# A two-layer decoder on one core: one more plain pair in block two, output rows for accumulating DMAs rounded in place in two buffers, and another order of the last pair's products

## The chip, the cores and the metric

The kernel runs on one core of a Trainium2 chip. The metric is the device time of one execution in microseconds (us), from several runs of the same program; lower is better. The engines are named as the profile names them: PE is TensorE (matrix products; PEld its weight loads), DVE is VectorE, ACT is ScalarE, POOL is GpSimd, SP is SyncE, which here only issues DMAs.

## The reference

One sequence of 256 tokens of width 2048 passes two layers. Each layer is a token mixer (mLSTM in layer one, a gated linear recurrence in layer two) and a feed-forward part; a final norm follows. All is float32. The change touches the feed-forward part alone, which is in both layers:

```python
def swiglu(x, w_in, w_out):            # w_in (2048, 2*5632), w_out (5632, 2048)
    g, u = jnp.split(x @ w_in, 2, axis=-1)
    return (jax.nn.silu(g) * u) @ w_out

h = h + swiglu(rms_norm(h, norm_ffn[layer]), ffn_w_in[layer], ffn_w_out[layer])
```

## The kernel before, in words

**Precision.** Every float32 operand is split into a rounded part `hi` (type float32r) and a remainder `lo`; each product is three matmuls, hi·hi, hi·lo and lo·hi (lines L829 to L831 of the profile). The split of weights is a cast on ACT (`hi`) and a subtraction on DVE (`lo`), lines L266 and L267.

**Blocks and pairs.** `ffn` cuts the 5632 hidden features into eleven blocks of 512 (`j` = 0 to 10 in names; the text calls them block one to eleven). A block streams the input weights as eight pairs of 128 rows (`p` = 0 to 7), 1 MB each, by SP (line L301) into three buffers. A pair is done in one of two ways. A *plain* pair is eight products: its weights are cast once (`whi`, 128x2048) and subtracted once (`wlo`). A pair *by sevens* uses Strassen's trick: four sums of weight quarters on DVE (`sum`, L310, L313, L314), then casts and remainders of the raw quarters (`whix`, `wlox`, 128x1536) and of the sums in two halves (`whit`, `wlot`, 128x1024 each), and seven products. The first half of the sums holds T1 and T3, the second T2 and T4; T2 is the third sum. Pair 0 of each block is plain; in block one pairs 1, 2, 3, 4 and 7 are plain as well (`BOTH`). For these the activations are kept in a second form, in a pool named `more`.

**The products** of a pair collect in seven PSUM banks: P1 (no sums), P2, Q3, Q5 (T1), P7 (T3), Q6 (T2), P4 (T4). The list `LAST` gives their order in the last pair of a block. At the block's end the banks are combined on ACT and DVE (L865 to L880) and gated: `ds` holds the results, `tv` and `hh` are their transposes, and the next block's first products need banks that these combinations have read.

**Output pieces.** Block j's result is multiplied with its 512 rows of the output weights while block j+1 runs: four quarters q of the columns, two token halves b, so eight pieces of twelve matmuls each, `out<j><q><b>`. They are taken up from pair 4 of the next block on, one for each pair, so pairs 1 to 3 of block two have none beside them. For a piece, `h` is copied into the one `out` bank (L949) and copied back when it is done (L960). The rows come as two halves i. For i = 0 SP loads them to `rawo`, and ACT and DVE split them. For i = 1 POOL loads them (L923), ACT writes `wlo` = −raw (L928), the tile type rounds it, POOL issues a second DMA that *adds* the unrounded rows from memory (L929), so that the remainder is left, and ACT casts raw to `whi` (L930). Before the change raw and `whi` of i = 1 are separate tiles with one buffer each, `wlo` has two.

**What sets the order.** The code is written in source order, but a scheduler lays the instructions of each engine in a fixed sequence when the program is built; each engine then runs its sequence strictly in order, and waits where an operand or a buffer is missing.

Of the kernel before, what the change touches and what calls it, by code (L numbers as in the profile page):

```python
# [8 lines left out]
F32 = mybir.dt.float32  # L9
F32R = mybir.dt.float32r  # L10
AF = mybir.ActivationFunctionType
ALU = mybir.AluOpType
PSUM = bass.MemoryType.PSUM

P = 128
# [9 lines left out]
NB = 512  # L25
# [4 lines left out]
SEVENS = (1, 2, 3, 4, 5, 6, 7)  # L30

BOTH = (1, 2, 3, 4, 7)

SHIFT = 48
PRODUCTS = (
    ("P1", "A11", "B11"), ("P2", "A12", "B21"), ("Q3", "A3", "B22"),
    ("Q5", "A5", "T1"), ("P7", "A7", "T3"), ("Q6", "A6", "T2"), ("P4", "A22", "T4"),
)

LAST = tuple(sorted(PRODUCTS, key=lambda c: ("P1", "Q6", "P7", "Q5", "P2", "Q3", "P4").index(c[0])))  # L40
SEVEN = ("A12", "A22", "A11", "A5", "A7", "A6", "A3")


# [1 line left out]
def kernel(  # L45
# [21 lines left out]
    nc = tc.nc  # L67
# [16 lines left out]
    def pool_of(key):  # L84
        return pools[key][0]
# [4 lines left out]
    def bank(tag, name):  # L90
        return pool_of("acc").tile([P, NB], F32, tag=tag, name=name)
# [90 lines left out]
    for part, (c, c0, srcs) in enumerate(parts):  # L182
        at = 0
# [81 lines left out]
    def split(hi, lo, src):  # L265
        nc.scalar.copy(hi, src)  # L266
        nc.vector.tensor_tensor(lo, src, hi.bitcast(F32), op=ALU.subtract)  # L267
# [19 lines left out]
                yield kg + i, *both[i]  # L287

    def is_plain(j, p):
        return p not in SEVENS or j == 0 and p in BOTH  # L290

    def pairs(w, j, held):

# [158 lines left out]
    class NormPairs(Norm):  # L452
# [10 lines left out]
        def pair(self, p):  # L463
# [21 lines left out]

            rest = SHIFT if p == NK // 2 - 1 else 0
            xt = pool_of("x").tile([P, 2 * n * P + rest], F32R, tag=f"p{p}", name=f"p{p}_{self.name}")
# [318 lines left out]
    NP = NK // 2  # L806

    def ffn(layer, n, nxt):
# [19 lines left out]
        def product(o, a, b, start, stop, **kw):  # L828
            nc.tensor.matmul(o, lhsT=a[0], rhs=b[0], start=start, stop=False, **kw)  # L829
            nc.tensor.matmul(o, lhsT=a[0], rhs=b[1], start=False, stop=False, **kw)  # L830
            nc.tensor.matmul(o, lhsT=a[1], rhs=b[0], start=False, stop=stop, **kw)  # L831

        def inner(j, between):

            ps = {}

            def add(c, a, b, stop):
                first = c not in ps
                if first:
                    ps[c] = bank(c, f"{c}_{j}")  # L840
                product(ps[c], a, b, first, stop)


            ds = fp.tile([P, 4, NB], F32, tag="ds", name=f"ds{j}")
            d0, d1, s0, s1 = (ds[:, i, :] for i in range(4))
            last = max(p for p in SEVENS if not is_plain(j, p))
            for p, ops in pairs(w, j, layer == 1):
                if is_plain(j, p):

                    work = [  # L850
                        (c, n.plain(p, f)[a], ops[2 * side + f], p == NP - 1 and f == 1)
                        for c, side, a in (("Q5", 1, 1), ("P2", 0, 0), ("Q3", 1, 2), ("P4", 0, 1)) for f in range(2)
                    ]
                else:
                    seven = n.seven(p)
                    work = [
                        (c, seven[a], ops[b], p == (last if c in ("P7", "P1", "Q6") else NP - 1))
                        for c, a, b in (LAST if p == NP - 1 else PRODUCTS)
                    ]
                for i, job in enumerate(work):  # L860
                    add(*job)
                    between(j, p, i + 1 - len(work))
                if p == last:
                    with tc.high_priority(offset=AHEAD):
                        nc.scalar.copy(s0, ps["P1"])  # L865
                        nc.vector.tensor_tensor(d0, ps["Q6"], s0, op=ALU.subtract)

                        nc.vector.tensor_tensor(d1, d0, ps["P7"], op=ALU.subtract)
            with tc.high_priority(offset=AHEAD):

                nc.vector.tensor_tensor(
                    ds[:, 0:4:3, :], ps["Q5"].unsqueeze(1).broadcast_to([P, 2, NB]), ds[:, 0:2, :], op=ALU.add
                )
                nc.vector.tensor_tensor(s0, ps["P2"], s0, op=ALU.add)
                nc.scalar.activation(s0, s0, AF.Silu, scale=n.rstd[:, 0:1])
                nc.vector.tensor_tensor(d0, ps["Q3"], d0, op=ALU.add)
                nc.vector.tensor_tensor(d1, ps["P4"], d1, op=ALU.subtract)
                nc.scalar.activation(d1, d1, AF.Silu, scale=n.rstd[:, 1:2])
                for b, (u, g) in enumerate(((d0, s0), (s1, d1))):
                    nc.vector.scalar_tensor_tensor(  # L880
                        out=u, in0=u, scalar=n.rstd[:, b:b + 1], in1=g, op0=ALU.mult, op1=ALU.mult
                    )
            return d0, s1
# [10 lines left out]

        fresh, copies = [True], []

        def outs(j, hi, lo):

            wv = ffn_w_out[layer][j * NB:(j + 1) * NB, :].rearrange("(k p) n -> p k n", p=P)
            held = {}

            def load(q, last):
                held.clear() if not last else None
                tiles = held[q] = []
                if last:
                    raw = four("raw", f"o{j}{q}", F32, 2)
                    for i in (0, 2):  # L910
                        nc.sync.dma_start(raw[:, i:i + 2, :], wv[:, i:i + 2, q * NB:(q + 1) * NB])
                    with tc.high_priority(offset=AHEAD):
                        tiles.extend(halves(f"o{j}{q}", raw))
                    return
                for i in range(2):

                    spare = "1" if i and q % 2 else ""
                    raw, wh, wl = (
                        pool_of(f"{what}o{at}").tile([P, 2, NB], dt, tag=f"{what}{i}", name=f"{what}o{j}{q}{i}")
                        for what, dt, at in (("raw", F32, ""), ("whi", F32R, ""), ("wlo", F32R, spare))  # L920
                    )
                    src = wv[:, 2 * i:2 * i + 2, q * NB:(q + 1) * NB]
                    (nc.gpsimd if i else nc.sync).dma_start(raw, src)  # L923
                    with tc.high_priority(offset=AHEAD):
                        if i:

                            with after(*copies[-2:-1]):
                                nc.scalar.activation(wl, raw, AF.Copy, scale=-1.0)  # L928
                            nc.gpsimd.dma_start(wl, src, accum_op=ALU.add)  # L929
                            nc.scalar.copy(wh, raw)  # L930
                        else:
                            split(wh, wl, raw)
                    tiles.extend((wh[:, k, :], wl[:, k, :]) for k in range(2))

            def piece(q, b, last=False):
                if b == 0:
                    load(q, last)
                tiles = held[q]
                bs = slice(b * P, (b + 1) * P)
                hs = h[:, b, q * NB:(q + 1) * NB]  # L940
                name = f"out{j}{q}{b}"
                o = acc(name) if last else pool_of("out").tile([P, NB], F32, tag="out", name=name)


                ends = q == 3 and last and nxt.lag and j == NJ - 1
                first = False if ends else last or fresh.pop() if last or fresh else False
                if not first:
                    with tc.high_priority(offset=AHEAD):
                        nc.scalar.copy(o, hs)  # L949
                for k in range(4):  # L950
                    product(o, (hi[:, k, bs], lo[:, k, bs]), tiles[k], first and k == 0, k == 3, skip_group_check=True)
                if ends:

                    nxt.store(b, o)
                    return
                with tc.high_priority(offset=AHEAD):
                    if first:
                        nc.vector.tensor_tensor(hs, o, hs, op=ALU.add)
                    else:
                        copies.append(nc.scalar.copy(hs, o))  # L960

            return [(piece, q, b) for q in range(4) for b in range(NT)]

        work, turns, late = [], [], []
# [13 lines left out]

        for j in range(NJ):
            v = inner(j, between)  # L980
            if j == 0:
                close_pools("more")
                open_pool("h1", f"h1_f{layer}")
            both = (pool_of("h1") if j % 2 else fp).tile([P, 2, 4, T], F32R, tag=f"h{j % 2}", name=f"hh{j}")
            hi, lo = both[:, 0], both[:, 1]
            turns.extend(lambda v=v, i=i, hi=hi, lo=lo: turn_v(v, i, hi, lo) for i in range(2))
            late.append(lambda j=j, hi=hi, lo=lo: outs(j, hi, lo))
        turn["raw"] %= 2
        for i, (piece, q, b) in enumerate(work):
            piece(q, b, i >= 2)  # L990
# [239 lines left out]
```

## Time and profile before

| what | value |
|---|---|
| median of three runs | 2095.55 us (2094.19 to 2095.74) |
| the profiled execution | 2094.86 us, of which 2093.1 us is the span from first to last instruction |
| PE clock granted | 0.998 |
| feed-forward part of layer one, blocks one to eleven | from 398 us to 1100 us of the span |
| feed-forward part of layer two | from 1390 us to 2093 us |

The profile's span is 1.76 us shorter than the execution's own time; the execution itself is 0.69 us under the median. Matmul records show 0.39 us each, but they are pipelined: the distance of two starts is what one costs.

### The profile page before, as it was taken

The page shows a single profiled execution, that of the slowest core. Times are in us where ns is not written, and L with a number is a line of the kernel's source. Part 1 is how long each engine was busy: PE and PEld are TensorE (multiplying, and loading weights), DVE is VectorE, ACT ScalarE, POOL GpSimd, SP SyncE. Part 2 cuts the span into 40 slices and gives each one's busy share as a digit, 9 for nine tenths or more (in the row PEclk, how much of TensorE's full clock was granted, in tenths as well). Part 3 has the DMA queues.
Part 4 walks back from the last instruction along what each step waited for, and adds up shares of the span by engine and source line. Part 5 has one row for each costly group of instructions (what it writes and reads, how often), then busy time and mean ns, then how long its engine had stood idle before and what let it go on. Part 6 is the DMA issues. An engine that isn't in the chain of part 4 may idle for free.

```text
span 2093.1 us, 27909 instructions
## 1 busy us (share of the span) xinstructions
PE 2068.5 (99%) x10424; PEld 1738.0 (83%) x10424; DVE 1746.0 (83%) x1930; ACT 1429.0 (68%) x1739; POOL 195.9 (9%) x218
## 2 busy tenths in 40 slices
PE   9999999999999999999999999999999999999998
PEld 8988888877888888888879999887788888888886
DVE  6655556699999999999976787669999999999995
ACT  5444455567777777877864778556787777887775
POOL 0011110000111111111100000000011111111112
PEclk9999999999999999999999999999999999999999
DMA  7556667656878878888765666665787888888784
GB/s 229 170 162 180 181 177 225 187 178 202 254 223 251 234 223 250 241 237 237 224 197 155 191 190 187 219 214 175 218 243 231 242 232 240 242 228 245 231 238 153
DMA packets 223135, 446.66 MB, mean 213 GB/s; under 512 B 16328, under 2 KB 17048, under 8 KB 222872
## 3 DMA queue, kind: packets, MB, share of 16 engines
q1 hardware_dynamic: 189832, 362.02, 53.5%
q0 software_dynamic: 32448, 81.80, 18.1%
q8 instruction: 81, 1.33, 0.3%
q10 hardware_dynamic: 720, 1.07, 0.1%
q14 instruction: 54, 0.44, 0.1%
HBM read 442.74 MB, written 2.10 MB: 213 GB/s over the span
## 4 chain that ended last, share of the span: by engine, by line
PE 73%; DVE 11%; issue 6%; ACT 4%; DMA 4%; POOL 1%; SPq 0%; ACTq 0%; POOLq 0%; DVEq 0%
PE out L829 5%; PE out L830 5%; PE out L831 5%; PE P L830 5%; PE P L831 5%; PE P L829 5%; PE Q L829 4%; PE Q L830 4%; PE Q L831 4%; DMA rawo<-in_ffn_w_out_dram 3%; DVE wlot L267 2%; DVE wlox L267 2%; PE po L328 2%; PE po L327 2%; PE po L326 2%
## 5 line engine op out<-in xcount | busy, mean ns | idle before, releaser
L266 ACT CAST whit<-sum 128x1024 fp32r<-128x1024 f32 x288 | 301.3, 1050 | 182.4 <-DVE sum L310 144.2
L242 DVE TENSOR_TENSOR wlo<-raw,whi 128x1024 fp32r<-128x1024 f32 (+1 forms) x226 | 273.5, 1213 | 172.3 <-ACT whi L241 169.8
L267 DVE TENSOR_TENSOR wlot<-sum,whit 128x1024 fp32r<-128x1024 f32 x288 | 348.9, 1221 | 36.0 <-ACT whit L266 34.6
L241 ACT CAST whi<-raw 128x1024 fp32r<-128x1024 f32 (+1 forms) x226 | 234.5, 1042 | 193.6 <-PE po L328 40.4
L829 PE MATMUL out<-whio,hh 128*128 128x512 f32 x704 | 275.5, 392 | 1.0 <-ACT hh L543 0.5
L830 PE MATMUL out<-wloo,hh 128*128 128x512 f32 x704 | 273.9, 390 | 0.0
L831 PE MATMUL out<-whio,hh 128*128 128x512 f32 x704 | 273.6, 390 | 0.0
L267 DVE TENSOR_TENSOR wlox<-raw,whix 128x1536 fp32r<-128x1536 f32 x144 | 252.5, 1753 | 23.4 <-ACT whix L266 23.0
L266 ACT CAST whix<-raw 128x1536 fp32r<-128x1536 f32 x144 | 213.6, 1483 | 25.4 <-PE P L831 24.2
L310 DVE TENSOR_TENSOR sum<-raw 128x1024 f32<-128x1024 f32 x144 | 176.2, 1223 | 3.9
L929 POOL DMA_DIRECT2D wloo<-in_ffn_w_out_dram x78 | 94.0, 1205 | 702.9 <-ACT wloo L928 678.2
L829 PEld LDWEIGHTS out<-whio,hh 128*128 128x128 f32 x704 | 132.2, 188 | 30.7 <-ACT out L949 1.7
L830 PEld LDWEIGHTS out<-wloo,hh 128*128 128x128 f32 x704 | 132.2, 188 | 28.2 <-DVE wloo L267 0.7
L831 PEld LDWEIGHTS out<-whio,hh 128*128 128x128 f32 x704 | 132.1, 188 | 27.8
L960 ACT COPY h<-out 128x512 f32<-128x512 f32 x154 | 89.8, 583 | 65.3 <-PE out L831 65.2
L923 POOL DMA_DIRECT2D rawo<-in_ffn_w_out_dram x78 | 59.1, 758 | 755.3 <-ACT whio L930 362.6
L267 DVE TENSOR_TENSOR wloo<-rawo,whio 128x1024 fp32r<-128x1024 f32 (+1 forms) x88 | 117.9, 1339 | 4.4 <-ACT whio L266 4.4
L829 PE MATMUL Q<-whit,p_f 128*128 128x512 f32 x288 | 113.9, 400 | 5.2 <-ACT whit L266 4.5
L830 PE MATMUL P<-wlox,p_f 128*128 128x512 f32 x288 | 113.3, 393 | 4.0 <-DVE wlox L267 3.8
L829 PE MATMUL P<-whix,p_f 128*128 128x512 f32 x288 | 112.3, 398 | 2.7 <-ACT whix L266 2.7
L830 PE MATMUL P<-wlot,p_f 128*128 128x512 f32 x288 | 112.6, 391 | 1.7 <-DVE wlot L267 1.7
L830 PE MATMUL Q<-wlot,p_f 128*128 128x512 f32 x288 | 113.2, 397 | 0.1
(296 smaller groups left out, 5240.9 us busy)
## 6 DMA issues: line engine op xcount, KB each, us to landing
raw<-in_ffn_w_in_dram SPq DMA_DIRECT2D x352, 512.0 KB, 4.8
rawo<-in_ffn_w_out_dram SPq DMA_DIRECT2D x98, 512.0 KB, 6.0
raw<-in_m_w_in_dram SPq DMA_DIRECT2D x94, 512.0 KB, 3.8
rawo<-in_ffn_w_out_dram POOLq DMA_DIRECT2D x78, 512.0 KB, 5.9
wloo<-in_ffn_w_out_dram POOLq DMA_DIRECT2D x78, 512.0 KB, 6.4
raw<-in_r_w_in_dram SPq DMA_DIRECT2D x64, 512.0 KB, 3.9
raw<-in_m_w_out_dram SPq DMA_DIRECT2D x32, 512.0 KB, 3.7
raw<-in_r_w_out_dram SPq DMA_DIRECT2D x32, 512.0 KB, 4.2
```

The costliest lines, as they stand in the source:

```text
L241: nc.scalar.copy(hi[:, i:i + step, 0:ncols], r)
L242: nc.vector.tensor_tensor(lo[:, i:i + step, 0:ncols], r, hi[:, i:i + step, 0:ncols].bitcast(F32), op=ALU.subtract)
L266: nc.scalar.copy(hi, src)
L267: nc.vector.tensor_tensor(lo, src, hi.bitcast(F32), op=ALU.subtract)
L310: nc.vector.tensor_tensor(t[:, 0:2, :], raw[:, 1:3, :], raw[:, 3:4, :].broadcast_to([P, 2, NB]), op=ALU.add)
L326: nc.tensor.matmul(o, lhsT=ah[:, bs], rhs=hi, start=(k == 0), stop=False)
L829: nc.tensor.matmul(o, lhsT=a[0], rhs=b[0], start=start, stop=False, **kw)
L830: nc.tensor.matmul(o, lhsT=a[0], rhs=b[1], start=False, stop=False, **kw)
L831: nc.tensor.matmul(o, lhsT=a[1], rhs=b[0], start=False, stop=stop, **kw)
L923: (nc.gpsimd if i else nc.sync).dma_start(raw, src)
L929: nc.gpsimd.dma_start(wl, src, accum_op=ALU.add)
L960: copies.append(nc.scalar.copy(hs, o))
```

## The change

Four things are changed in `ffn`; nothing else is.

1. `SECOND = (3,)`: pair 3 of block two (`j` = 1) becomes plain. Its activations come from `more`, so that pool stays open one block longer.
2. `LAST`: the last pair's products go P1, P2, Q5, P7, Q6, Q3, P4 instead of P1, Q6, P7, Q5, P2, Q3, P4, so T2, the third sum, is wanted fifth and not second. A plain pair begins with P2 instead of Q5. As P2 is now early, the sum of P1 and P2 is made before Q6 is read, and P1 is copied out twice (`s0` and `d0`).
3. For the rows i = 1 the raw tile and `whi` are one buffer: the DMA writes it, ACT makes `wlo` from it and then rounds it in place. There are two such buffers, for even and odd q.
4. At each layer's first block two one-element copies on POOL hold the first loads of output rows until the first block's result exists.

```diff
+SECOND = (3,)
...
-LAST = tuple(sorted(PRODUCTS, key=lambda c: ("P1", "Q6", "P7", "Q5", "P2", "Q3", "P4").index(c[0])))
+LAST = tuple(sorted(PRODUCTS, key=lambda c: ("P1", "P2", "Q5", "P7", "Q6", "Q3", "P4").index(c[0])))
...
     def is_plain(j, p):
-        return p not in SEVENS or j == 0 and p in BOTH
+        return p not in SEVENS or j == 0 and p in BOTH or j == 1 and p in SECOND
...
-                        for c, side, a in (("Q5", 1, 1), ("P2", 0, 0), ("Q3", 1, 2), ("P4", 0, 1)) for f in range(2)
+                        for c, side, a in (("P2", 0, 0), ("Q5", 1, 1), ("Q3", 1, 2), ("P4", 0, 1)) for f in range(2)
...
                         nc.scalar.copy(s0, ps["P1"])
-                        nc.vector.tensor_tensor(d0, ps["Q6"], s0, op=ALU.subtract)
+                        first = s0
+                        if p == NP - 1:
+
+                            first = d0
+                            nc.scalar.copy(d0, ps["P1"])
+                            nc.vector.tensor_tensor(s0, ps["P2"], s0, op=ALU.add)
+                        nc.vector.tensor_tensor(d0, ps["Q6"], first, op=ALU.subtract)
...
-                nc.vector.tensor_tensor(s0, ps["P2"], s0, op=ALU.add)
+                if last < NP - 1:
+                    nc.vector.tensor_tensor(s0, ps["P2"], s0, op=ALU.add)
...
-                    spare = "1" if i and q % 2 else ""
-                    raw, wh, wl = (
-                        pool_of(f"{what}o{at}").tile([P, 2, NB], dt, tag=f"{what}{i}", name=f"{what}o{j}{q}{i}")
-                        for what, dt, at in (("raw", F32, ""), ("whi", F32R, ""), ("wlo", F32R, spare))
-                    )
...
-                    (nc.gpsimd if i else nc.sync).dma_start(raw, src)
+                    if i == 0:
+                        raw, wh, wl = buffer("raw", F32, ""), buffer("whi", F32R, ""), buffer("wlo", F32R, "")
+                    else:
+
+                        wh, wl = buffer(("raw", "whi")[q % 2], F32R, ""), buffer("wlo", F32R, ("", "1")[q % 2])
+                        raw = wh.bitcast(F32)
+                    if j == 0 and q == 0:
+
+                        nc.gpsimd.tensor_copy((wh if i else raw)[0:1, 0, 0:1], v[0][0:1, 0:1])
+                    (nc.gpsimd if i else nc.sync).dma_start(wh if i else raw, src)
...
-            if j == 0:
+            if j == 1:
                 close_pools("more")
                 open_pool("h1", f"h1_f{layer}")
```

Lines after L33 stand two to sixteen lower in the changed kernel: the three matmuls are L831 to L833 there, the cast L268, the DMA of rows L939, the negation L944, the adding DMA L945, the rounding in place L946, the `out` copies L965 and L976, and the block's end L867 to L889.

The scheduler lays the junctions of two blocks anew. The three places below are of the junction from block seven (names with 6) to block eight (names with 7) in layer one, with the third quarter (q = 2) of block six's output rows: tiles `520` (i = 0) and `521` (i = 1).

ACT, before, from the last pair's first sum cast to the copy into the bank of piece `out520`:

```order
L266 CAST whit6_7_6877<-sum6_7_6869 128x1024
L960 COPY h_73<-out510_6845 128x512
L928 ACTIVATE wloo521_6968<-rawo521_6966 128x1024
L266 CAST whit6_7_6877<-sum6_7_6869 128x1024
L949 COPY out511_6895<-h_73 128x512
L865 COPY ds6_6428<-P1_6_6523 128x512
L266 CAST whi7_0_6935<-raw7_0_6932 128x2048
L266 CAST whio520_6961<-rawo520_6960 128x1024
L960 COPY h_73<-out511_6895 128x512
L930 CAST whio521_6967<-rawo521_6966 128x1024
L949 COPY out520_6973<-h_73 128x512
```

ACT, now, the same stretch:

```order
L268 CAST whit6_7_6855<-sum6_7_6847 128x1024
L976 COPY h_73<-out510_6823 128x512
L268 CAST whit6_7_6855<-sum6_7_6847 128x1024
L965 COPY out511_6873<-h_73 128x512
L867 COPY ds6_6410<-P1_6_6504 128x512
L872 COPY ds6_6410<-P1_6_6504 128x512
L268 CAST whi7_0_6914<-raw7_0_6911 128x2048
L884 ACTIVATE ds6_6410<-ds6_6410,rstd_f0_3779 128x512
L268 CAST whio520_6940<-rawo520_6939 128x1024
L944 ACTIVATE wloo521_6946<-rawo521_6945 128x1024
L976 COPY h_73<-out511_6873 128x512
L946 CAST rawo521_6945<-rawo521_6945 128x1024
```

The negation of `521` (L928, now L944) has moved from the third row to the tenth: behind the copies of P1, the next block's first cast, an activation and the cast of `520`.

POOL, before, the DMAs of rows i = 1 around it (`rawo` loads, `wloo` adds):

```order
L929 DMA wloo511_6840<-in_ffn_w_out_dram 128x2x512
L923 DMA rawo521_6966<-in_ffn_w_out_dram 128x2x512
L929 DMA wloo521_6968<-in_ffn_w_out_dram 128x2x512
L923 DMA rawo531_7103<-in_ffn_w_out_dram 128x2x512
L929 DMA wloo531_7105<-in_ffn_w_out_dram 128x2x512
```

POOL, now (`rawo` and `whio` are the two buffers that are loaded and rounded in place):

```order
L945 DMA wloo511_6818<-in_ffn_w_out_dram 128x2x512
L939 DMA rawo521_6945<-in_ffn_w_out_dram 128x2x512
L939 DMA whio531_7081<-in_ffn_w_out_dram 128x2x512
L945 DMA wloo521_6946<-in_ffn_w_out_dram 128x2x512
L945 DMA wloo531_7082<-in_ffn_w_out_dram 128x2x512
```

The load of the following quarter, `531`, stands ahead of the adding DMA of `521`. This pair of rows is turned in this way for the third quarter of blocks one, two, four, six and eight, in both layers; for blocks three, five, seven and nine it stands as before, and there L944 stands ahead of the second sum cast.

PE, before, where the adding DMA's result is first read (`out520<-wloo521`); Q3 and P4 are products of block eight's pair 0. The piece's six matmuls on `520` and the first on `521` stand thirteen rows further up, ahead of the twelve of Q5 and Q3:

```order
L829 MATMUL Q3_7_6953<-whi7_0_6935,p0_f0_3097 128x512
L830 MATMUL Q3_7_6953<-wlo7_0_6936,p0_f0_3097 128x512
L831 MATMUL Q3_7_6953<-whi7_0_6935,p0_f0_3097 128x512
L830 MATMUL out520_6973<-wloo521_6968,hh5_6427 128x512
L831 MATMUL out520_6973<-whio521_6967,hh5_6427 128x512
L829 MATMUL out520_6973<-whio521_6967,hh5_6427 128x512
```

PE, now, from the end of P2 of block eight's pair 0 on:

```order
L833 MATMUL P2_7_6918<-whi7_0_6914,p0_f0_3097 128x512
L831 MATMUL out520_6951<-whio520_6940,hh5_6409 128x512
L832 MATMUL out520_6951<-wloo520_6941,hh5_6409 128x512
L833 MATMUL out520_6951<-whio520_6940,hh5_6409 128x512
L831 MATMUL out520_6951<-whio520_6940,hh5_6409 128x512
L832 MATMUL out520_6951<-wloo520_6941,hh5_6409 128x512
L833 MATMUL out520_6951<-whio520_6940,hh5_6409 128x512
L831 MATMUL out520_6951<-rawo521_6945,hh5_6409 128x512
L831 MATMUL P1_7_7004<-whix7_1_6994,p1_f0_3118 128x512
L832 MATMUL out520_6951<-wloo521_6946,hh5_6409 128x512
L833 MATMUL out520_6951<-rawo521_6945,hh5_6409 128x512
L831 MATMUL Q5_7_6925<-whi7_0_6914,p0_f0_3097 128x512
```

The read of `wloo521` now comes eight matmuls after P2, ahead of Q5 and Q3, which follow it.

More of the change, by code (lines that the diff above doesn't have):

```diff
@@ L895, in ffn, with outs @@
         fresh, copies = [True], []
-        def outs(j, hi, lo):
+        def outs(j, hi, lo, v):
             wv = ffn_w_out[layer][j * NB:(j + 1) * NB, :].rearrange("(k p) n -> p k n", p=P)
@@ L915, in load, with buffer @@
                 for i in range(2):
-                    spare = "1" if i and q % 2 else ""
-                    raw, wh, wl = (
-                        pool_of(f"{what}o{at}").tile([P, 2, NB], dt, tag=f"{what}{i}", name=f"{what}o{j}{q}{i}")
-                        for what, dt, at in (("raw", F32, ""), ("whi", F32R, ""), ("wlo", F32R, spare))
-                    )
-                    src = wv[:, 2 * i:2 * i + 2, q * NB:(q + 1) * NB]
-                    (nc.gpsimd if i else nc.sync).dma_start(raw, src)
+                    src = wv[:, 2 * i:2 * i + 2, q * NB:(q + 1) * NB]
+                    def buffer(what, dtype, at):
+                        return pool_of(f"{what}o{at}").tile([P, 2, NB], dtype, tag=f"{what}{i}", name=f"{what}o{j}{q}{i}")
+                    if i == 0:
[6 more added lines that the diff above has]
+                    (nc.gpsimd if i else nc.sync).dma_start(wh if i else raw, src)
                     with tc.high_priority(offset=AHEAD):
@@ L986, in ffn @@
             turns.extend(lambda v=v, i=i, hi=hi, lo=lo: turn_v(v, i, hi, lo) for i in range(2))
-            late.append(lambda j=j, hi=hi, lo=lo: outs(j, hi, lo))
+            late.append(lambda j=j, hi=hi, lo=lo, v=v: outs(j, hi, lo, v))
         turn["raw"] %= 2
```

## Prediction

> **What bounds the kernel now.** I read the page first, for the engine that is never idle.
>
> ```profile
> PE 2068.5 (99%) x10424; PEld 1738.0 (83%) x10424; DVE 1746.0 (83%) x1930; ACT 1429.0 (68%) x1739; POOL 195.9 (9%) x218
> ```
>
> PE is busy 99% of the span, so only two things change the time: matmuls added or taken away, and gaps between them. A busy PE hides gaps, so I next take the distance of two starts from the timeline.
>
> ```profile
> 814.55 0.39 PE L831 MATMUL out<-whio,hh 128*128 128x512 f32 x1
> 814.78 0.39 PE L829 MATMUL out<-whio,hh 128*128 128x512 f32 x1
> ...
> 450.83 0.60 PE L889 MATMUL tv<-ident,ds 128*128 128x128 f32 x4
> 451.19 0.48 PE L829 MATMUL P<-whix,p_f 128*128 128x512 f32 x1
> ```
>
> One matmul costs 0.227 us; four transposes 0.36. A block from the second on has 24 matmuls in its plain pair, 147 in seven pairs by sevens, 96 in eight output pieces: 267 x 0.227 + 0.8 for transposes = 61.4 us without a gap. Against this floor I hold windows from pair 4 of one block to pair 4 of the next: block two to three, then the eight after it, in each layer (columns: window, its length, busy us and instructions of PE, PEld, DVE, ACT, POOL, granted clock, DMA share, GB/s).
>
> ```profile
> 465.63:534.54 68.91, 66.24 (x283) 50.95 (x281) 65.82 (x65) 48.89 (x56) 5.86 (x6) 1.00 0.72 211
> 534.54:1031.06 496.52, 494.71 (x2202) 406.36 (x2200) 471.21 (x458) 386.70 (x442) 62.89 (x65) 1.00 0.82 237
> 1456.50:1525.41 68.91, 66.23 (x283) 50.98 (x282) 65.81 (x65) 48.90 (x56) 5.86 (x6) 1.00 0.71 211
> 1525.41:2021.13 495.72, 494.55 (x2201) 406.24 (x2200) 471.36 (x458) 386.52 (x442) 62.87 (x65) 1.00 0.82 238
> ```
>
> The eight blocks take 62.07 us each in layer one (496.52/8) and 61.97 in layer two: 5.3 and 4.5 us over the floor in all. Block two's window holds about 6 matmuls more (283 against 277), 1.4 us, and is 68.91 - 61.4 - 1.4 = 6.1 us over it. The longest total of the weight loads' waits (us, times, longest), over the whole span, names who is late:
>
> ```profile
> PEld Q L829 <- ACT whit L266: 15.4, 26, 2.0
> ```
>
> Q waiting for `whit` is Q6 in the last pair, where T2 is wanted second: in the window of the eight blocks this wait is
>
> ```profile
> PEld Q L829 <- ACT whit L266: 5.1, 8, 0.9
> ```
>
> once for each block. So before the change PE is the bound, DVE follows closely (471/496 = 95%), and the feed-forward parts lose some 6 us twice in block two and about 10 in last pairs.
>
> **Part A, pair 3 of block two plain.** DVE's work for one pair by sevens, in block two:
>
> ```profile
> 454.20 1.22 DVE L310 TENSOR_TENSOR sum<-raw 128x1024 f32<-128x1024 f32 x1
> ...
> 459.34 1.75 DVE L267 TENSOR_TENSOR wlox<-raw,whix 128x1536 fp32r<-128x1536 f32 x1
> 461.01 1.22 DVE L267 TENSOR_TENSOR wlot<-sum,whit 128x1024 fp32r<-128x1024 f32 x1
> 462.15 1.22 DVE L267 TENSOR_TENSOR wloo<-rawo,whio 128x1024 fp32r<-128x1024 f32 x1
> ```
>
> From 454.20 to 462.15, less the next pair's `wlox` (1.67), is 6.28 us; PE needs 21 x 0.227 = 4.77 for the pair while no output piece stands beside it. Pairs 1 to 3 so put DVE 3 x 1.5 = 4.5 us behind, and DVE is 65.82/68.91 = 96% busy while PE waits. A plain pair costs DVE one subtraction:
>
> ```profile
> L267 DVE TENSOR_TENSOR wlo<-raw,whi 128x2048 fp32r<-128x2048 f32 x32 | 73.0, 2286 | 15.2 <-ACT whi L266 15.2
> ```
>
> 2.2 us with overlap instead of 6.28, and PE one product more, 3 x 0.227 = 0.68. After two pairs by sevens DVE is 3.0 behind, and gains 5.44 - 2.2 = 3.2 in the plain one: the deficit is gone when the pieces begin. Of the 6.1 us I leave 0.7 for what is not DVE's, and pay 0.68: **-4.7 us a layer, -9.4 in both**; between -3 and -5.4 each.
>
> **Part B, T2 wanted later.** The wait for `whit` goes from all last pairs; its worth is 5.3 + 4.5 us, and block eleven of layer one has the longest of these waits, 2.0, of which I count 1.7: -11.5. What is late next? Piece `out511` needs its copy-in (L949, now L965) 2.72 us after the last pair's start. Where L944 now stands ahead of the second sum's cast (four junctions a layer) that copy comes about 0.95 later than without it, some 0.5 past the need, and the next block's plain remainder 0.3 later. I give back 0.8 for these eight and 0.2 for the other ten: 8.4. **B = -3 us**, between -11.5 (nothing given back) and +3 (1.4 and 0.35, as the junction's DVE work of block end, `wlo` and sums leaves little room).
>
> **Part C, the adding DMA.** This is the large term. At ten junctions (five a layer) L944 has moved behind the next block's casts, while PE reads the result eight matmuls after P2. Clock: start of P1 in the last pair, at the junction of blocks seven and eight
>
> ```profile
> 804.35 0.39 PE L829 MATMUL P<-whix,p_f 128*128 128x512 f32 x1
> ```
>
> PE reads `wloo521` after P1, P2, Q5, P7 (12 matmuls), a piece (12), Q6, Q3, P4 (9), P2 of the next block (6), seven of the next piece and one of P1: 47 x 0.227 = **10.7 us**. ACT before, same junction:
>
> ```profile
> 803.72 1.06 ACT L928 ACTIVATE wloo<-rawo 128x1024 fp32r<-128x1024 f32 x1
> ...
> 806.75 0.58 ACT L865 COPY ds<-P 128x512 f32<-128x512 f32 x1
> 807.22 1.92 ACT L266 CAST whi<-raw 128x2048 fp32r<-128x2048 f32 x1
> ...
> 810.95 0.59 ACT L960 COPY h<-out 128x512 f32<-128x512 f32 x1 [0.36 <-PE out L831]
> 811.43 1.05 ACT L930 CAST whio<-rawo 128x1024 fp32r<-128x1024 f32 x1
> 812.38 0.59 ACT L949 COPY out<-h 128x512 f32<-128x512 f32 x1
> 812.90 0.72 ACT L875 ACTIVATE ds<-ds,rstd_f 128x512 f32<-128x512 f32 x1
> 813.53 1.47 ACT L266 CAST whix<-raw 128x1536 fp32r<-128x1536 f32 x1
> ```
>
> Each next one starts about 0.1 before the shown end. Now ahead of L944 stand, from the first copy of P1: two copies 0.47 each, `whi` 1.82, the activation 0.63, `whio` 0.95, and L944 itself 1.06: 5.4 us. The copy of P1 can't start before P1 is done. A bank is read 0.25 after the next product's start (this row against 810.95 above):
>
> ```profile
> 810.70 0.39 PE L829 MATMUL P<-whix,p_f 128*128 128x512 f32 x1
> ```
>
> so 0.68 + 0.25 = 0.93 at the earliest, and 806.75 - 804.35 = 2.4 as now. I take 1.4, nearer the early end, because T2's cast no longer has L928 ahead of it. L944 then ends at 6.8. POOL's row and the landings of all 78 adding DMAs:
>
> ```profile
> 805.09 1.20 POOL L929 DMA_DIRECT2D wloo<-in_ffn_w_out_dram  x1 [6.80 <-ACT wloo L928]
> ...
> DMA to landing us min/median/max: 6.0/6.4/9.5
> ```
>
> Issue is 0.3 behind L928's end (804.78): 7.1. Just ahead of it POOL now issues the next load (when the piece has left its buffer: 24 x 0.227 + 0.25 = 5.7), so two transfers of 512 KB are close together. The nearest row is 409 us, where a load followed an adding DMA after 0.9 us:
>
> ```profile
> wloo<-in_ffn_w_out_dram POOLq DMA_DIRECT2D x1, 512.0 KB, 8.1
> rawo<-in_ffn_w_out_dram POOLq DMA_DIRECT2D x1, 512.0 KB, 9.1
> ```
>
> I take 7.0, between the median and these: landing at 14.1, and PE waits 14.1 - 10.7 = **3.4 us**. Bounds: 0.93 + 5.4 + 0.3 + 6.0 = 12.6, a wait of 1.9; 2.4 + 5.4 + 0.3 + 9.5 = 17.6, a wait of 6.9. Behind the waiting matmul stand Q5, Q3 and P4 of pair 0 and the transposes; PE works in order, so nothing fills the gap. **C = 10 x 3.4 = +34 us**, 19 to 69 at the ends. Before, L928 at 803.72 let POOL issue at 805.09, and the data were there by 814.6 even with the longest landing; PE asked at 818.40:
>
> ```profile
> 818.40 0.39 PE L830 MATMUL out<-wloo,hh 128*128 128x512 f32 x1
> ```
>
> so this term is wholly new.
>
> [...] With the median of 6.4 instead, C would be 28.
>
> **Other edits.** Rounding in place (L946) is the same cast as L930. The two small POOL copies hold the first output rows until `ds` exists; SP's half was issued earlier before:
>
> ```profile
> 447.80 0.75 DVE L880 SCALAR_TENSOR_TENSOR ds<-ds,rstd_f 128x512 f32<-128x512 f32 x1
> ...
> 435.84 0.37 SPq L923 DMA_DIRECT2D rawo<-in_ffn_w_out_dram  x1
> ```
>
> Issued near 448.6 and landing in 9.1 at most by the rows above, they are there at 457.7; their remainder on DVE stood at 462.15: nothing. If that cover failed, ACT would queue behind L944 of block one and A would be lost.
>
> **Sum.** 2094.86 (the profiled execution) - 9.4 - 3 + 34 = 2116.5, say **2116 us**; the median of the runs before is 0.7 above that execution.
>
> **Rivals.** *The add lands in time* (faster). It decides at 10.7 - 7.1 = 3.6 us from issue to landing. Then only A and B are left: 2094.9 - 12.4 = 2082. For it: two buffers let the raw rows come earlier, and the wait before was nil. Against it: 6.0 is the least of 78. Chance 0.17.
>
> [...]
>
> *The wait is real but small.* PE reaches the read late anyway, because the copy-in of `out520` and the block-end sums are late, and 1.2 us of wait at each of the ten cancels A and B: 2095. Chance 0.08. *A does not come*: ACT holds block two's casts behind the late first rows, +9.4: 2126. Chance 0.05.
>
> **How the numbers follow.** The forecast has 0.70, with waits of 2.2 to 5 us: 2104 to 2133 with A and B as taken. Slower: 0.70 + 0.05 = 0.75; within 0.2% (4.2 us, what a measurement can tell): 0.08; faster 0.17. To leave out no more than 2 in 10 the range runs from 2080 to 2134.
>
> **What would show it.** In the profile after: PE waits for DMA `wloo` at the `lo` matmul of `out`, ten times, 2 to 5 us each, and windows of about 65 us at every other block. Q waiting for `whit` nearly gone, block two's window near 64 us with its wait on the add. If those ten waits are missing, C is wrong and the time falls to about 2082; if block two's window keeps its excess beside the wait, A is.

## The result, and the profile after

| | before | changed |
|---|---|---|
| median of five runs | 2095.74 us (2094.19 to 2096.12) | 2184.80 us (2184.30 to 2185.67) |
| ratio, 95% interval | 1 | 1.0426 (1.0411 to 1.0442) |
| span of the profiled execution | 2093.1 us | 2182.4 us |
| mean clock granted to PE | 0.998 | 0.976 |

The kernel is 89 us slower. Slower was forecast, but by 21 us, and 2184.8 lies far outside the range of 2080 to 2134. The page's row of busy times, and the two longest totals among PE's waits (us, times, longest):

```profile
PE 2088.9 (96%) x10430; PEld 1761.3 (81%) x10430; DVE 1736.0 (80%) x1920; ACT 1435.8 (66%) x1755; POOL 205.8 (9%) x222
```

```profile
PE out L832 <- DMA wloo<-in_ffn_w_out_dram: 69.0, 10, 7.5
PE Q L831 <- ACT whit L268: 9.7, 4, 4.6
```

The ten waits for the adding DMA are there, at the ten places named, with 6.9 us each instead of 3.4. The second row is a new wait. For the weight loads, which wait first, the old loss of the last pairs is gone: Q for `whit` was 15.4 us in 26 waits; now it is 11.3 in 4, and nearly all of that are the two waits of block two in the second row above. Three windows of one block each (columns as in the prediction), the first and third with a late negation at the junction:

```profile
675.12:746.67 71.55, 64.67 (x277) 52.84 (x275) 57.82 (x57) 48.48 (x56) 7.72 (x8) 0.93 0.74 210
746.67:808.28 61.61, 61.61 (x276) 50.85 (x275) 59.63 (x59) 48.88 (x57) 7.75 (x8) 1.00 0.79 233
808.28:879.72 71.44, 64.63 (x276) 52.86 (x275) 57.84 (x57) 48.53 (x56) 7.71 (x8) 0.93 0.74 212
```

The middle one is 0.2 us over the floor of 61.4; the first and the third are 9.9 and 9.8 us longer than it. PE idles 6.9 and 6.8 us in them (length less busy), so 3 us of the loss lie in time that counts as busy, and the clock column says where: 0.93 instead of 1.00. The timeline of PE at the junction from block seven to eight, from the last pair's start to the read and behind it:

```profile
830.72 0.39 PE L831 MATMUL P<-whix,p_f 128*128 128x512 f32 x1
...
841.18 0.39 PE L831 MATMUL P<-whix,p_f 128*128 128x512 f32 x1
848.38 0.79 PE L832 MATMUL out<-wloo,hh 128*128 128x512 f32 x1 [6.81 <-DMA wloo<-in_ffn_w_out_dram]
848.97 0.63 PE L833 MATMUL out<-rawo,hh 128*128 128x512 f32 x1
849.39 0.63 PE L831 MATMUL Q<-whi,p_f 128*128 128x512 f32 x1
...
854.51 0.44 PE L833 MATMUL Q<-whi,p_f 128*128 128x512 f32 x1
854.79 0.39 PE L831 MATMUL Q<-whi,p_f 128*128 128x512 f32 x1
```

Behind the wait two starts stand 0.43 us apart, not 0.227, until 854.5: 14 distances that take 6.13 us (854.51 - 848.38) where 3.18 would do. Windows of that stretch and of the next (the clock is the third column from the end):

```profile
848.38:854.80 6.42, 6.42 (x16) 5.02 (x17) 0.00 (x0) 1.27 (x2) 0.00 (x0) 0.52 0.37 143
854.80:861.20 6.40, 6.40 (x34) 5.37 (x33) 5.45 (x6) 5.76 (x8) 1.19 (x1) 1.00 0.54 82
```

So PE was granted half its clock after the wait, 0.52 in the first window, and 1.00 in the second. ACT and POOL at the same junction, and the landings of what was issued from 836.8 to 839.5 us (the last number, from issue to landing; `raw` are SP's loads of input weights, `rawo` by SP is the other half of the next quarter):

```profile
836.42 1.07 ACT L944 ACTIVATE wloo<-rawo 128x1024 fp32r<-128x1024 f32 x1
...
836.88 0.72 POOL L939 DMA_DIRECT2D whio<-in_ffn_w_out_dram  x1 [14.47 <-ACT whio L268]
837.80 1.21 POOL L945 DMA_DIRECT2D wloo<-in_ffn_w_out_dram  x1 [0.20 <-issue]
```

```profile
raw<-in_ffn_w_in_dram SPq DMA_DIRECT2D x2, 512.0 KB, 5.8
whio<-in_ffn_w_out_dram POOLq DMA_DIRECT2D x1, 512.0 KB, 5.3
wloo<-in_ffn_w_out_dram POOLq DMA_DIRECT2D x1, 512.0 KB, 10.5
rawo<-in_ffn_w_out_dram SPq DMA_DIRECT2D x1, 512.0 KB, 9.4
```

The negation ended at 837.49, 6.77 us after the last pair's start (forecast 6.8); the add was issued at 7.08 (7.1); PE came to the read at 841.4, 10.7 (10.7). Only the landing is off: 10.5 us, not 7.0. At the ten places it is 9.8 to 11.3 us, 10.5 on average. Over all 78 adds:

```profile
DMA to landing us min/median/max: 5.9/7.5/11.3
```

The second new wait is in block two. POOL, ACT and PE there, in layer one:

```profile
445.07 0.49 POOL L938 COPY rawo<-ds 1x1 f32<-1x1 f32 x1 [38.06 <-DVE ds L889]
445.51 5.24 POOL L938 CAST rawo<-ds 1x1 fp32r<-1x1 f32 x1
451.06 0.75 POOL L939 DMA_DIRECT2D rawo<-in_ffn_w_out_dram  x1 [0.30 <-POOL rawo L938]
...
455.87 1.06 ACT L944 ACTIVATE wloo<-rawo 128x1024 fp32r<-128x1024 f32 x1 [4.61 <-DMA rawo<-in_ffn_w_out_dram]
...
457.91 1.04 ACT L268 CAST whit<-sum 128x1024 fp32r<-128x1024 f32 x1
...
459.00 0.79 PE L831 MATMUL Q<-whit,p_f 128*128 128x512 f32 x1 [4.37 <-ACT whit L268]
```

Read from below: PE waits for a cast, which stands behind the negation of block one's first row, which waits for a load, which POOL issues only after one element has taken 5.24 us to cast.

### The profile page after: what moved, and what is told of

The parts are those of the page before. It is cut to its first block, busy times and chain, and to the rows that moved or that the text cites. A ratio compares the mean times of both kernels' runs of the same rounds, so it can differ in the third digit from the quotient of the medians.

```text
span 2182.4 us, 27890 instructions
## 1 busy us (share of the span) xinstructions
PE 2088.9 (96%) x10430; PEld 1761.3 (81%) x10430; DVE 1736.0 (80%) x1920; ACT 1435.8 (66%) x1755; POOL 205.8 (9%) x222
## 4 chain that ended last, share of the span: by engine, by line
PE 82%; DMA 6%; issue 6%; DVE 2%; ACT 2%; POOL 1%; POOLq 0%; ACTq 0%; SPq 0%; DVEq 0%
PE out L832 7%; PE out L833 7%; PE out L831 6%; PE P L832 6%; PE P L833 6%; PE P L831 5%; DMA wloo<-in_ffn_w_out_dram 5%; PE Q L831 5%; PE Q L832 5%; PE Q L833 5%; PE po L328 3%; PE po L330 3%; PE po L329 3%; PE v L328 1%; PE o L330 1%
## 5 line engine op out<-in xcount | busy, mean ns | idle before, releaser
L268 ACT CAST whit<-sum 128x1024 fp32r<-128x1024 f32 x284 | 296.3, 1052 | 153.9 <-DVE sum L312 147.8
L832 PE MATMUL out<-wloo,hh 128*128 128x512 f32 x704 | 281.6, 400 | 69.1 <-DMA wloo<-in_ffn_w_out_dram 69.0
L268 ACT CAST whix<-raw 128x1536 fp32r<-128x1536 f32 x142 | 210.7, 1484 | 37.6 <-PE P L833 32.8
L831 PE MATMUL out<-whio,hh 128*128 128x512 f32 x544 | 212.6, 391 | 1.5 <-ACT whio L268 1.2
L833 PE MATMUL out<-whio,hh 128*128 128x512 f32 x544 | 211.5, 390 | 0.7 <-DVE hh L546 0.7
L976 ACT COPY h<-out 128x512 f32<-128x512 f32 x154 | 89.9, 584 | 169.7 <-PE out L833 169.1
L945 POOL DMA_DIRECT2D wloo<-in_ffn_w_out_dram x78 | 93.3, 1197 | 723.3 <-ACT wloo L944 691.5
L831 PEld LDWEIGHTS out<-whio,hh 128*128 128x128 f32 x544 | 102.1, 188 | 25.4 <-ACT out L965 2.4
L831 PE MATMUL Q<-whit,p_f 128*128 128x512 f32 x284 | 111.5, 393 | 9.7 <-ACT whit L268 9.7
L833 PEld LDWEIGHTS out<-whio,hh 128*128 128x128 f32 x544 | 102.1, 188 | 22.1 <-DVE hh L546 1.1
L268 ACT CAST whio<-rawo 128x1024 fp32r<-128x1024 f32 (+1 forms) x88 | 101.2, 1150 | 18.9 <-PE out L833 16.8
L833 PE MATMUL P<-whix,p_f 128*128 128x512 f32 x284 | 113.2, 398 | 0.0
L831 PE MATMUL P<-whit,p_f 128*128 128x512 f32 x284 | 111.2, 392 | 0.0
L831 PE MATMUL P<-whix,p_f 128*128 128x512 f32 x284 | 111.0, 393 | 0.0
```

## The experiments

All ratios are against the kernel before on the same chip, with 95% intervals; 0.001 of it is 2.1 us.

**The second edit alone.** The kernel before with the new `LAST`, the new order of plain pairs and the later sum.

```diff
-LAST = ... ("P1", "Q6", "P7", "Q5", "P2", "Q3", "P4")
+LAST = ... ("P1", "P2", "Q5", "P7", "Q6", "Q3", "P4")
```

> The kernel before with the second edit alone: the last pair's new order and the third sum wanted later; rows are still loaded into a tile of their own, and block two's pairs are as before. In the order of the program the negation still stands behind the next block's casts at ten junctions (here before blocks two, three, five, seven and nine of each layer), and the load of the last quarter now comes BEHIND the adding DMA, since the one raw tile has to be read first. Theory 1 (the late negation, and the add queued behind the load just ahead of it in its queue): the ten waits stay but shrink, since the add lands 6.0 to 8.4 us after its issue instead of 10.5: waits of 2.4 to 4.8 us, up to 3 us more each where the clock halves after a gap, with 15 us of gain at the other junctions: 2105 to 2160 us. Theory 2 (late negation, but the landing is long because all queues are full just then): landing near 10.5 again, waits near 7 us with 3 us of slow clock each, 2175 to 2190 us. Theory 3 (the rows loaded in place cause the waits, not the order): no such waits, 2080 to 2090 us.

Ratio 1.0394 (1.0378 to 1.0409), 2177.5 us. PE's waits, and the add of one junction, issued at 767.65:

```profile
PE out L830 <- DMA wloo<-in_ffn_w_out_dram: 57.4, 10, 6.3
```

```profile
wloo<-in_ffn_w_out_dram POOLq DMA_DIRECT2D x1, 512.0 KB, 9.0
rawo<-in_ffn_w_out_dram POOLq DMA_DIRECT2D x1, 512.0 KB, 9.6
rawo<-in_ffn_w_out_dram SPq DMA_DIRECT2D x1, 512.0 KB, 9.3
```

The order alone makes ten such waits, 5.7 us each, at other junctions than in the changed kernel (rows of blocks two, three, five, seven and nine); rows rounded in place are not needed for them (theory 3 falls). Here the load of the next quarter is issued behind the add, and the ten landings are 8.7 to 9.7 us: less than 10.5, but far above 6.0. So that this load stands ahead is a small part of the length.

**The first edit alone.** Pair 3 of block two plain, nothing else.

```diff
+SECOND = (3,)
-        return p not in SEVENS or j == 0 and p in BOTH
+        return p not in SEVENS or j == 0 and p in BOTH or j == 1 and p in SECOND
```

> The kernel before with the first edit alone: pair three of block two plain, nothing else. Theory 1: the term of the prediction holds where nothing else is moved: 4.7 us per layer, 2086 us (2084 to 2089). Rival: block two's loss is not the conversion of that pair but whatever comes behind it, and the gain is given back there: 2093 to 2097 us, with the loss in block two near 6.5 us as before.

Ratio 0.9968 (0.9955 to 0.9981), 6.7 us faster (4.0 to 9.4). Windows from the first product of layer one's feed-forward part to P2 of pair 4 in block three, of the kernel before and then of this one:

```profile
397.50:534.54 137.04, 132.12 (x568) 104.14 (x568) 121.62 (x124) 90.17 (x97) 10.73 (x11) 0.99 0.69 209
```

```profile
397.73:530.13 132.40, 129.80 (x570) 105.80 (x571) 118.29 (x120) 89.50 (x96) 11.35 (x12) 0.99 0.70 214
```

137.04 - 132.40 = 4.6 us in layer one; the same windows of layer two give 135.04 - 130.58 = 4.5. The forecast said 4.7 for each.

**The third edit with the fourth.** Rows for adding DMAs in place in two buffers, the first of them held by POOL; nothing else.

> The kernel before with the third edit alone: rows for adding DMAs rounded in place in two buffers in turn, the first of them held back by the one-element copies, the pool of the early block kept open one block longer; the old order of the last pair, block two as before. Theory 1: this edit alone places the first row's negation of a layer late and ACT stands there until block one's result is there; that costs the wait of 4.6 us in block two with the slow clock behind it (7 us) in each layer where the negation lies ahead of block two's casts, and nothing elsewhere: 2095 to 2110 us. Rival (in-place rows double the packets of the loads, 42432 against 32448, and slow every add): adds land 1 us later at all places, but with slacks of 1.8 us or more in the order that shows nowhere: 2094 to 2097 us with no wait of a Q matmul for a cast in block two.

Ratio 1.0051 (1.0034 to 1.0068), 10.7 us slower. The adds land as before (6.3 us in the middle, against 6.4), so the rival falls. PE waits in block two behind the same cast of 5.25 us:

```profile
445.48 5.25 POOL L931 CAST rawo<-ds 1x1 fp32r<-1x1 f32 x1
...
459.79 0.80 PE L831 MATMUL Q<-whit,p_f 128*128 128x512 f32 x1 [5.16 <-ACT whit L268]
```

**The changed kernel with the negation early.**

```diff
-                            with after(*copies[-2:-1]):
+                            with after(*copies[(-3 if q == 2 else -2):(-2 if q == 2 else -1)]):
```

> The changed kernel with one edit: the negation of the third quarter's second half may be issued one copy earlier, so that it stands behind the copy before, ahead of the next block's casts, at every junction (the kernel has it there at the early junctions only). Everything else as changed. Theory 1 (the ten waits and the slow clock behind them are the whole of the loss beyond block two): ten times 10.2 us go, 2184.8 - 102 = 2083 us (2078 to 2090), no wait of an out matmul for an adding DMA left. Rival (the later third sum or the in-place rows cost something that the waits cover): 2095 us or more. If the adds still land late for another reason (the queue): waits remain, 2120 to 2180 us.

Ratio 0.9973 (0.9962 to 0.9984), 2089.8 us. Against 1.0426 that is 95 us less (0.0453 x 2095). The longest total of PE's waits:

```profile
PE Q L831 <- ACT whit L268: 10.5, 4, 5.0
```

No wait for an adding DMA is left in the list; next comes one of 2.2 us. The place of one instruction on ACT, ten times, makes 95 us of the loss; block two's wait stays.

**The hold on ACT.** The kernel of the last run, with the negation early, and the one-element write of the first row i = 1 made by ACT.

```diff
-                        nc.gpsimd.tensor_copy((wh if i else raw)[0:1, 0, 0:1], v[0][0:1, 0:1])
+                        (nc.scalar.copy if i else nc.gpsimd.tensor_copy)((wh if i else raw)[0:1, 0, 0:1], v[0][0:1, 0:1])
```

> The kernel with the negation early, and one edit more: the one-element write that holds back the first row for an adding DMA is made by ACT instead of POOL. In the trace of the kernel with the negation early POOL's write of that one element takes 5.24 us (444.58 to 449.82; the one beside it, with no change of type, 0.49), the load is issued 0.3 us later, lands at 455.47, ACT stands 5.2 us at the negation, and PE waits 5.0 us for the cast behind it, with the halved clock for another 2.5. Theory (those 5.2 us are real and set block two's loss): the load starts 5 us earlier, block two's loss falls from 9.9 and 9.1 us to under 2, 2089.8 - 15.6 = 2074 us (2072 to 2079). Rival (the span of a copy on POOL is rough, and the load's start is set by block one's result all the same): 2086 to 2092 us, with the wait of a Q matmul for a cast still near 5 us.

Ratio 0.9906 (0.9892 to 0.9921), 2078.6 us beside 2098.8 for the kernel before on that chip: 14 us below the one with the negation early, by the ratios (each uncertain by 2 to 3 us). POOL and ACT in block two:

```profile
445.51 0.48 POOL L938 COPY rawo<-ds 1x1 f32<-1x1 f32 x1 [38.05 <-DVE ds L889]
445.95 0.75 POOL L939 DMA_DIRECT2D rawo<-in_ffn_w_out_dram  x1
...
445.38 0.19 ACT L938 CAST rawo<-ds 1x1 fp32r<-1x1 f32 x1
...
453.24 1.06 ACT L944 ACTIVATE wloo<-rawo 128x1024 fp32r<-128x1024 f32 x1 [1.48 <-DMA rawo<-in_ffn_w_out_dram]
```

The write takes ACT 0.19 us, the load starts 0.44 us behind the start of POOL's first copy instead of 5.99 (451.06 - 445.07 in the changed kernel), and ACT waits 1.5 us for it.

**The second edit with the negation early, on the kernel before.** The edit of `LAST` and that of `after` together; rows still in a tile of their own.

> The kernel before with the second edit alone (last pair's order, third sum later), and the negation allowed one copy earlier. What the later sum is worth where no add lands late. By the term of the prediction (11.5 us of waits go, 8.4 come back): 2095 - 3 = 2092 us (2090 to 2093). By the kernel with the negation early, whose blocks three to ten lose 0.4 to 0.6 us each where before they lost 0.6 to 1.5, with the two ends of a layer some us better: 2095 - 9 = 2086 us (2083 to 2089).

Both expectations missed: ratio 1.0189 (1.0174 to 1.0204). ACT's waits in this kernel, then in the kernel before:

```profile
ACT wloo L935 <- DMA rawo<-in_ffn_w_out_dram: 104.9, 41, 8.8
```

```profile
ACT wloo L928 <- DMA rawo<-in_ffn_w_out_dram: 23.5, 11, 8.7
```

With a single raw tile the row can't be loaded before the last one is read, so a negation that stands early waits on ACT, and the casts behind it come late. With the third edit in place (the kernel with the negation early) ACT's waits for the loads of these rows are 17.6 us in all. So that edit is what lets the negation stand early; I take it that the second buffer does it, which was not tried by itself.

**First and second edit with the negation early**, also without the two buffers and the holds.

> The first and the second edit, with the negation early, and without the third edit (rows loaded into a tile of their own, as before). If the two gains add: the time of the run before it in this list less the 7 to 9.6 us of the plain pair; 2077 us if the later sum is worth 9, 2084 us if it is worth 3. If they hinder each other (DVE is the engine that both relieve): 2086 us or more.

Ratio 1.0153 (1.0134 to 1.0171): 7.5 us less than without the plain pair (1.0189 - 1.0153), with ACT's wait for rows as long as there (110.9 us). For what the later sum is worth neither run serves.

**The add ahead of the next load.** The changed kernel, that load ordered behind the add on POOL.

> The changed kernel with one edit: the load of the last quarter's second half is issued behind the adding DMA of the third quarter, not ahead of it; by this the negation stands late at nearly every junction (some 16 to 18 instead of ten), so what counts is the single wait. Theory 1 (the add is queued behind that load and its landing is the load's landing plus 6): landing 6 to 7 us, waits of 2.4 to 3.4 us, nearly no halved clock. Theory 2 (the landing is long since the loads of SP run at the same time, whatever the order, as in the kernel with the order alone, where it took 8.7 to 9.7): landing 8.7 to 9.7, waits of 5 to 6 us and 2 to 3 us of halved clock each.

2226.2 us in one run. Eighteen waits, and the landing of one of the adds (issue at 846.02):

```profile
PE out L832 <- DMA wloo<-in_ffn_w_out_dram: 103.6, 18, 6.8
```

```profile
wloo<-in_ffn_w_out_dram POOLq DMA_DIRECT2D x1, 512.0 KB, 9.0
```

8.8 to 10.3 us over the eighteen, 9.2 in the middle; waits of 5.4 to 6.8. Theory 2 holds for nearly all of the length; that the load stands ahead accounts for 1.3 us.

**The old order again**, in the kernel with the hold on ACT.

> The kernel with the hold on ACT and the negation early, with the second edit undone: the last pair's old order and the old place of the third sum (the negation then stands early without help, as before). So: the plain pair, the rows in two buffers, the hold on ACT. The difference to the kernel with the hold on ACT is what the later sum is worth when no add lands late. By the term of the prediction (11.5 us of waits go, 8.4 come back): 3 us slower than that kernel, ratio to before 0.992. By the losses of the blocks (three to ten lose 0.4 to 0.6 us each there, 0.6 to 1.5 before, and the two ends of a layer 3 us more): 9 to 12 us slower, ratio 0.995 to 0.996. If the old order was better than thought: no difference.

Ratio 0.9954 (0.9937 to 0.9971), against 0.9906 with the later sum: 10 us, each ratio uncertain by 3 to 3.5, so 5 to 15. The weight loads' waits for `whit` here, then with the later sum:

```profile
PEld Q L831 <- ACT whit L268: 12.4, 23, 2.7
```

```profile
PEld Q L831 <- ACT whit L268: 3.3, 3, 1.8
```

**No hold on the first row i = 1 at all**, negation early.

> As the kernel with the hold on ACT, but the first row for an adding DMA isn't held back at all (only the row that SP loads is): its load starts far earlier, before block one's result is there. Theory (POOL's 5.2 us and the hold are all of block two's extra loss): ratio as with the hold on ACT, 0.990 to 0.991, block two's loss between 1.5 and 4.3 us. Rival (without the hold the load takes the place of a transfer that block one needs, and PE waits there): ratio 0.993 or more, with a new wait for a raw tile in block one.

Ratio 0.9914 (0.9899 to 0.9929): the same as with the hold on ACT, with no new wait in block one.

**Both loads of the last quarter behind the landed add.**

> The changed kernel with both loads of the last quarter held back until the adding DMA of the third quarter has landed (a one-element write by POOL that reads the added tile stands ahead of each), in all blocks. The negation is as late as in the changed kernel at the same ten places. What counts is the landing of the ten adds (10.5 us in the changed kernel, 9.2 with only the order in its queue turned round), not the total, since the next adds come later too. Theory 2 (the loads that run beside it share the transfer's time): with two of the four loads beside it gone, 6.5 to 8 us, waits of 2.8 to 4.5 us. Theory 3 (an add that is issued right behind a late negation is slow for another reason, the loads have no part): still 9 us or more.

The ten adds land 7.9 to 8.2 us after their issue, and the longest wait is 4.8 us. Here is the add issued at 837.62, and what SP issues within 0.3 us of it:

```profile
raw<-in_ffn_w_in_dram SPq DMA_DIRECT2D x2, 512.0 KB, 4.1
wloo<-in_ffn_w_out_dram POOLq DMA_DIRECT2D x1, 512.0 KB, 8.0
```

So the landing goes down as its neighbours go: 10.5 with the POOL load ahead and three loads of SP beside it, 9.2 with the POOL load behind, 8.0 with both loads of the last quarter away and SP's two loads of input weights still beside it. Theory 3 falls. With nothing issued near it, at 855.38 us of the changed kernel, it is

```profile
wloo<-in_ffn_w_out_dram POOLq DMA_DIRECT2D x1, 512.0 KB, 5.9
```

That the last 2.1 us belong to the two loads of input weights is an inference from these two places; no run moved those loads.

The total, 2186.8 us, says nothing here, since other waits come in (13.0 us for `hh`).

**The cast twice.** The kernel with the negation early, POOL's one-element cast repeated.

> The kernel with the negation early (first row for an adding DMA still held by POOL's one-element cast), with that cast made twice in a row. Theory (a one-time cost of the first cast after other work on POOL, not of the element: at 1.6 us of the span POOL casts 8x1024 elements in 1.03 us): the first takes 5.2 us again, the second 0.5 to 1 us; PE's wait in block two grows by as much, from 5.0 to 5.5 to 6 us, and the total by 1 to 3 us from 0.9973 of before. Rival (each such cast costs 5.2 us): the load starts 5.2 us later, the wait is near 10 us, and the total is 10 us or more higher, 1.002 of before.

Ratio 0.9978 (0.9967 to 0.9989), beside 0.9973 with one cast. The two casts together, in layer one and in layer two, and the durations of all four (ns: least, median, longest; then the first and the last start in us):

```profile
444.78 5.49 POOL L939 CAST rawo<-ds 1x1 fp32r<-1x1 f32 x2
...
1431.17 5.49 POOL L939 CAST rawo<-ds 1x1 fp32r<-1x1 f32 x2
```

```profile
L939 POOL CAST rawo<-ds x4: 175/2710/5252, 444.8 to 1436.5; 1x1 fp32r<-1x1 f32 x4
```

Each pair is 5.25 and 0.175 us: the first costs, and a second right behind it doesn't. The rival is out. PE's longest wait did not grow with it (4.7 us instead of 5.0); 0.2 us are too little to show there.

## Why the prediction was off

**Part A, right in itself.** 4.7 us a layer were forecast, 4.6 and 4.5 measured when it is done alone. In the changed kernel it doesn't show, since block two has a loss of its own.

**Part B, mis-sized.** -3 was forecast: -11.5 and 8.4 given back through later `out` copies. Measured are -10 (-5 to -15), near the end of my range at which nothing comes back. The weight loads' waits for that copy in the changed kernel (us, times, longest):

```profile
PEld out L831 <- ACT out L965: 2.4, 10, 0.7
```

It was 1.7 before: 0.7 us given back, not 8.4. In the eight blocks that follow, where the prediction expected most of it, the kernel with the negation early and the hold on ACT has no such wait. These blocks from pair 4 of block three on, in that kernel:

```profile
529.82:1022.28 492.46, 492.46 (x2202) 406.74 (x2200) 470.28 (x457) 391.97 (x449) 62.09 (x64) 1.00 0.83 239
1509.86:2002.32 492.46, 492.46 (x2202) 406.74 (x2200) 470.29 (x457) 391.87 (x449) 62.09 (x64) 1.00 0.83 239
```

496.52 + 495.72 before, 984.92 here: 7.3 us, and the records show no idle time of PE in them (length and busy time are equal).

**Part C, the mechanism right, the price of one wait wrong.** At eight of the ten places the moment of the read, the end of the negation and the issue were met within 0.1 us; at the two of block one's rows the issue came half a microsecond later or more. The step that failed is "I take 7.0, between the median and these": 10.5 us was the landing, so 6.9 us of wait instead of 3.4. That 6.9 was also my upper bound is luck: the bound had 2.4 us for the copy of P1 and 9.5 for the landing, where 1.4 and 10.5 came. Even 69 us for C would have given only 2151 with A and B as taken. The neighbour I priced was one load of the same queue, from one pair of rows at 409 us. Of the added 4.5 us (10.5 against 6.0), 2.5 go with the two loads of the next quarter, one by POOL and one by SP, of which turning the order of POOL's two makes 1.3; the rest is there beside the two loads of input weights, which the sum didn't have either.

**A term was missing.** After each of the ten waits PE runs at half clock for 7 to 14 matmuls: 1.6 to 3.0 us, 26 us over the ten (each distance of starts above 0.3 us, less 0.227). The slow stretch lasted 3.1 to 6.1 us. The waits in block two have it too, 1.5 and 2.1 us. In the feed-forward parts of the changed kernel the gaps between starts of these twelve waits are 4.76 to 7.91 us, the others at most 1.5 us; all twelve are followed by half clock at once. In the kernel before, the longest gap there is 2.58 us (430.62 to 433.20): the clock stayed full for 1.5 us of work after that, and then was half:

```profile
433.30:434.55 1.25, 1.25 (x6) 1.03 (x7) 1.25 (x2) 1.25 (x2) 0.00 (x0) 1.00 0.33 34
434.70:438.00 3.30, 3.30 (x9) 2.60 (x8) 3.25 (x3) 2.04 (x2) 0.00 (x0) 0.50 0.96 354
```

The next longest gaps there are 1.2 to 2.0 us, and behind them the clock stayed full, as behind the one of 1.96 us from 1423.29 to 1425.25:

```profile
1425.30:1429.00 3.70, 3.70 (x16) 3.07 (x17) 3.70 (x4) 3.19 (x3) 0.00 (x0) 1.00 0.71 224
```

**"Nothing" for the POOL copies was wrong, by 11 to 14 us.** The load was there earlier than I had allowed for (issue at 451.06, ACT goes on at 455.87, against 457.7). But I compared it with the remainder on DVE at 462.15. The first reader is the negation, which stands on ACT ahead of a cast that PE wants at 454.6 (459.00 - 4.37). What I had named as the price if that cover failed (ACT queues behind L944, A is lost) is what came, together with C and not as a rival to it: the third and fourth edits alone cost 10.7 us, and moving one element's cast off POOL gives 14 back.

**The sum again.** By the ratios, step by step: -9.6 us from the kernel before to the one with the plain pair, the rows in two buffers, the hold on ACT and the old order (0.9954); -10.1 for the second edit, B (0.9906); 14.0 for the hold by POOL (0.9973); 94.9 for the late negation, C (1.0426). Together 89.2. These steps join end to end, so that they add up to the measured 89 proves nothing; each has its own error of some us. The first is near the -9.4 forecast for A, though it has the rows in it too. Of C, 69 are waits and 26 the clock. Against the forecast, C is 61 us more, the copies 14 more, and B 7 less.

## What to carry to other kernels

Where a change moves the start of a transfer closer to its reader, price its landing from transfers that have the same neighbours in all queues (here 10.5 us with four loads beside it, 5.9 with nothing issued near it), and ask what else was waiting for the moment that releases it. Add to such a wait on PE what the slow clock behind it cost: here 1.6 to 3.0 us behind waits of 6.9 us on average, 1.5 and 2.1 behind waits of 4.4 and 4.6. For each load that is held back, find its first reader on each engine, and what stands behind that reader in the engine's order: here ACT stood 4.61 us at the negation, and PE 4.37 at the product of the cast behind it.

The best version here has the first three edits, with the negation ahead of the next block's casts and the first row's hold on ACT: 0.9906 of the time before (0.9892 to 0.9921); with no hold on that row at all it is the same within the error.

## What the runs showed of the hardware

- A one-element cast on POOL took 5.24 us, and 0.175 us when made again right behind it; 986 us later the first took 5.25 us once more. A plain copy of one element beside it took 0.49. The same cast took ACT 0.19. POOL's first cast to float32r in the changed kernel's execution, 8x1024 elements at 1.6 us, took 1.03. What the 5.1 us between the first and the second cast are, no run shows.
- One adding DMA of 512 KB took from 5.9 to 11.3 us in the changed kernel; at the same place 10.5 became 8.0 when two of the loads beside it were held back.
- PE's clock was half from 434.7 to 438.0 us in the kernel before, behind a gap of 2.58 us between starts, and behind each of the twelve gaps of 4.76 to 7.91 us in the changed kernel; behind gaps of 1.2 to 2.0 us in the feed-forward parts of these two it was full.
